# A seven-product output projection for the first half of a hybrid decoder block

## The chip, the core and the metric

The kernel runs on one core of a Trainium2 chip. The core has TensorE (matrix products into PSUM), VectorE (DVE), ScalarE (ACT), GpSimd (POOL), and SyncE (SP), which here issues every DMA. The metric is the time of one execution on the device, in microseconds; less is better. Times are medians of several runs. The profile is one further execution, recorded instruction by instruction; its times count from its first instruction.

## The reference

One decoder layer over 2048 positions of width 1024, in float32:

```python
h = rmsnorm(x, norm1_g)
p_q, p_k, p_v, p_g, p_a, c_b, c_c, c_h = split(h @ w_in)
o_gla  = rmsnorm(gla_chunked(q, k, v, log_a), gla_norm_g) * silu(p_g)   # 512 columns
o_conv = c_b * causal_depthwise_conv(c_c * c_h, conv_w)                 # 512 columns
x = x + concatenate([o_gla, o_conv]) @ w_out                            # 1024 x 1024
h2 = rmsnorm(x, norm2_g)
x = x + (silu(h2 @ w_ffn_gate) * (h2 @ w_ffn_up)) @ w_ffn_down
return rmsnorm(x, norm_f_g)
```

`gla_chunked` is a causal gated linear attention with a state carried from chunk to chunk.

## The kernel before

**Precision.** TensorE multiplies a rounded form of float32. Each operand is therefore split into a high part and the rest: ACT writes the high part, DVE subtracts (`split`, L146 and L147). A product of two split operands is three matmuls: high by high, high by rest, rest by high (L328 to L330 in `product_step`).

**Seven products.** The positions are in four blocks of 512, two to a half. The large projections are done half by half in units. A unit takes a 2x2 arrangement of weight tiles (A11 to A22) and a 2x2 arrangement of operands: B11 and B12 are the first half of the depth for the two blocks, B21 and B22 the second. Instead of eight products it does seven, on sums and differences of weights (S1 to S4, made by POOL in `unit_weights`) and of operands:

- T1 = B12 - B11, T2 = B22 - T1, T3 = B22 - B12, T4 = B21 - T2.
- The order is A11 B11, S1 T1, S2 T2, A12 B21, S3 T3, S4 B22, A22 T4 (`PRODUCTS`).

At a depth of 1024 a product is four steps of 128, so twelve matmuls, and a unit 84. Of its four results three are collected in SBUF by ACT copies (L348) and DVE adds (L352); the fourth stays in PSUM.

**Stages.** In order: statistics and operands of half 0; input projection of half 0 (twelve units); input projection of half 1 (twelve units); output projection of half 0; output projection of half 1; then the FFN of each half. The operands of half 1 (28 of them, 512 KB each with both parts) are made in the background of the input projection of half 0 by `h1_ahead` and stored in DRAM (`s_h1`); `load_pairs` loads them when the second input projection begins. The pool `opp` holds 28 operands.

**The output projection** (`out_proj`, from L712) is plain: for each pair of output tiles, eight depth steps of 128, each with three matmuls for each tile and block (L722, L723, L725), so 384 for a half. Its operands are the GLA and conv results, split and stored as pairs (`s_gla`, `s_mix`), loaded by `build_mix`. DVE adds the residual, the sum is stored in `s_x1`, and `sum_squares` (L703, L704) gathers the statistics of the next norm. The residual tiles, the unit's copies and the squares come from one pool of nine buffers (`tp`).

**Order of the work.** `tick()` is called after every product, and after every depth step of the plain output projection. Every second tick takes one step from the queue `background` (gate, GLA chunks, operands of half 1); a flag `hurry` makes it every tick at the start. If a generator is in `ahead`, it gets a step at every fourth tick; before the FFN nothing is in it. A GLA chunk is three steps: scores, finish of the chunk before, outputs. `gla_half(0)` mostly runs in the input projection of half 1, `gate(1)` behind it, and `gla_half(1)` from there into the output projection. GLA tiles, gate tiles and operands under way share the pool `bx` of eleven buffers of 128x512. The set `done` names finished chunks, of each half only the last.

A planner simulates the program while it is built. It orders each engine's instructions, the DMA issues of SP included, by the times at which it expects them to be ready, and gives out buffers as they come free. On the chip each engine, and SP's queue, then goes through its instructions in that order.

The change touches the ends of these functions and the driver:

```python
for r, j, c, _ in next(units):                 # conv results, L568
    y = cc[r, j]
    dve.tensor_tensor(y[:], c[:], y[:], ALU.mult)
    hi = tp.tile([P, PB], F32R, name="hi", tag="t")
    split(y[:], hi[:], y[:].bitcast(F32R))
...
drain_background(lambda: (1, PT - 1) in done)  # driver, L980
ssq = out_proj(0, build_mix(0))
```

## Time and profile before

| | |
|---|---|
| median of 3 runs | 2166.09 us |
| lowest, highest | 2165.67, 2172.95 us |
| the profiled execution | 2172.21 us, span 2170.2 us |
| granted TensorE clock in it | 0.983 |
| TensorE busy | 95% |
| DVE, ACT, POOL busy | 67%, 46%, 46% |
| moved by DMA | 467.65 MB, 215 GB/s |

A row of the groups of instructions names the line, the engine, the operation, the tile it writes and those it reads, the shapes and the count; behind the bar stand the busy time in microseconds and the mean of one in nanoseconds, and then the idle time of the engine before them with what ended it. A row by stretch gives the stretch, its length, and for each engine the busy time and the number of instructions, then the granted clock, the share of the 16 DMA engines and GB/s. A row of the chain of waits gives a start, a length, and what the chain ran through. A DMA row ends with the median time from issue to landing. PE is TensorE's matmuls, PEld its weight loads.

### The profile page before, as it was taken

What the parts mean: (1) busy time and instruction counts of PE and PEld (TensorE: products, weight loads), DVE (VectorE), ACT (ScalarE), POOL (GpSimd) and SP (SyncE); (2) the same over time, 40 slices, a digit from 0 to 9 for tenths busy, and PEclk for the clock granted to TensorE, in tenths of its full rate; (3) what the DMA queues carried; (4) which work ended last, traced back from release to release, by engine and by line L of the source; (5) the groups of instructions that cost most, each with busy time, mean ns of one, the idle gap of its engine ahead of it and who ended that gap; (6) DMA issues with size and microseconds to landing.
All of it is one profiled execution on the core that took longest, in us unless ns stands there. A gap on an engine that the chain in (4) does not pass through costs nothing.

```text
span 2170.2 us, 26909 instructions
## 1 busy us (share of the span) xinstructions
PE 2055.1 (95%) x9133; PEld 1658.8 (76%) x9133; DVE 1447.5 (67%) x2034; ACT 1009.1 (46%) x1960; POOL 993.6 (46%) x714
## 2 busy tenths in 40 slices
PE   4899999999999999999999999998999999999896
PEld 3577787887888887788888877787888888876675
DVE  8849965557774486787887565554656666576654
ACT  4555434564543334554555453333444545463344
POOL 4526422212201374555555337774545444447774
PEclk9999999999999999999999999999999999999998
DMA  3259668532576882565555677698343534688772
GB/s 148 73 197 317 217 239 276 153 116 89 169 274 214 334 306 97 187 244 194 217 215 184 227 304 263 240 342 326 125 167 136 184 136 149 229 331 328 292 276 107
DMA packets 189978, 467.65 MB, mean 215 GB/s; under 512 B 19856, under 2 KB 65168, under 8 KB 180112
## 3 DMA queue, kind: packets, MB, share of 16 engines
q1 hardware_dynamic: 189840, 465.93, 59.5%
q8 instruction: 72, 1.18, 0.2%
q14 instruction: 66, 0.54, 0.1%
HBM read 297.03 MB, written 168.82 MB: 215 GB/s over the span
## 4 chain that ended last, share of the span: by engine, by line
PE 71%; DVE 11%; DMA 8%; issue 4%; ACT 3%; POOL 3%; SPq 1%; DVEq 0%; POOLq 0%; ACTq 0%
PE mm L328 21%; PE mm L330 21%; PE mm L329 20%; DVE wq L147 2%; DVE h L440 2%; DMA op<-sa_T 2%; PE mm L722 2%; PE mm L725 2%; PE mm L723 2%; DMA raw<-in_wdown_dram 1%; DVE op L147 1%; DMA op<-sa_B 1%; DVE so L147 1%; ACT wq L146 1%; DVE c L352 1%
## 5 line engine op out<-in xcount | busy, mean ns | idle before, releaser
L328 PE MATMUL mm<-op,wq 128*128 128x512 f32 x2495 | 987.7, 398 | 38.6 <-ACT c L348 18.2
L330 PE MATMUL mm<-op,wq 128*128 128x512 f32 x2495 | 972.0, 394 | 18.8 <-DVE wq L147 18.0
L329 PE MATMUL mm<-op,wq 128*128 128x512 f32 x2495 | 981.0, 393 | 4.1 <-DVE op L147 4.1
L147 DVE TENSOR_TENSOR wq<-raw,wq 128x512 fp32r<-128x512 f32 (+2 forms) x628 | 532.1, 854 | 345.0 <-ACT wq L146 338.9
L146 ACT ACTIVATE wq<-raw 128x512 fp32r<-128x512 f32 (+2 forms) x628 | 365.2, 587 | 583.4 <-PE mm L330 408.5
L328 PEld LDWEIGHTS mm<-op,wq 128*128 128x128 f32 x2495 | 473.4, 190 | 159.1 <-ACT c L348 25.4
L330 PEld LDWEIGHTS mm<-op,wq 128*128 128x128 f32 x2495 | 473.4, 190 | 130.4 <-DVE wq L147 30.7
L329 PEld LDWEIGHTS mm<-op,wq 128*128 128x128 f32 x2495 | 473.4, 190 | 102.3 <-DVE op L147 5.1
L313 POOL TENSOR_TENSOR raw<-s,raw 128x512 f32<-128x512 f32 (+2 forms) x98 | 131.8, 1345 | 473.6 <-DVE wq L147 442.8
L352 DVE TENSOR_TENSOR c<-mm,c 128x512 f32<-128x512 f32 x270 | 185.2, 686 | 101.2 <-PE mm L330 98.5
L311 POOL TENSOR_TENSOR s<-raw 128x512 f32<-128x512 f32 (+2 forms) x98 | 131.0, 1337 | 197.7 <-DMA raw<-in_wffn_dram 87.5
L318 POOL TENSOR_TENSOR raw<-raw 128x512 f32<-128x512 f32 (+2 forms) x98 | 129.9, 1326 | 128.9 <-DVE wq L147 119.8
L348 ACT ACTIVATE c<-mm 128x512 f32<-128x512 f32 x270 | 156.7, 585 | 31.3 <-PE mm L330 30.2
L312 POOL TENSOR_TENSOR raw<-raw 128x512 f32<-128x512 f32 (+2 forms) x98 | 138.0, 1409 | 4.7
L704 POOL TENSOR_TENSOR ssx<-ssx,q 128x512 f32<-128x512 f32 x52 | 75.7, 1467 | 136.4 <-ACT q L703 136.1
L884 POOL TENSOR_TENSOR y<-c,y 128x512 f32<-128x512 f32 x66 | 98.9, 1500 | 72.4 <-DVE c L352 68.9
L147 DVE TENSOR_TENSOR so<-t,so 128x512 fp32r<-128x512 f32 x100 | 87.9, 885 | 26.0 <-ACT so L146 25.8
L146 ACT ACTIVATE wq<-s 128x512 fp32r<-128x512 f32 (+2 forms) x98 | 57.5, 587 | 94.5 <-PE mm L330 91.8
L722 PE MATMUL mm<-op,wq 128*128 128x512 f32 x256 | 101.1, 395 | 0.0
L723 PE MATMUL mm<-op,wq 128*128 128x512 f32 x256 | 99.8, 390 | 0.0
L147 DVE TENSOR_TENSOR wq<-s,wq 128x512 fp32r<-128x512 f32 (+2 forms) x98 | 77.6, 792 | 17.0 <-ACT wq L146 16.4
L146 ACT ACTIVATE so<-t 128x512 fp32r<-128x512 f32 x100 | 62.8, 629 | 42.8 <-DMA sa_T<-so 17.6
(177 smaller groups left out, 1922.8 us busy)
## 6 DMA issues: line engine op xcount, KB each, us to landing
raw<-in_wffn_dram SPq DMA_DIRECT2D x44, 1024.0 KB, 5.4
sa_T<-so SPq DMA_DIRECT2D x88, 512.0 KB, 4.7
op<-sa_T SPq DMA_DIRECT2D x88, 512.0 KB, 9.8
sa_B<-so SPq DMA_DIRECT2D x69, 512.0 KB, 3.4
op<-sa_B SPq DMA_DIRECT2D x69, 512.0 KB, 9.6
raw<-in_win_dram SPq DMA_DIRECT2D x24, 1024.0 KB, 5.3
raw<-in_wdown_dram SPq DMA_DIRECT2D x24, 768.0 KB, 6.6
sx<-y SPq DMA_DIRECT2D x48, 256.0 KB, 3.5
```

Of the source, the lines that this page charges most:

```text
L146: last_hi[:] = [act.activation(hi, src, AF.Copy)]
L147: return dve.tensor_tensor(lo, src, hi.bitcast(F32), ALU.subtract)
L311: pool.tensor_tensor(s1, a21, a22, ALU.add)
L312: pool.tensor_tensor(a21, a11, a21, ALU.subtract)
L313: pool.tensor_tensor(a11, s1, a11, ALU.subtract)
L328: pe.matmul(o[:], wh, xh, start=first and k == 0, stop=False, skip_group_check=True)
L329: pe.matmul(o[:], wh, xl, start=False, stop=False, skip_group_check=True)
L330: return pe.matmul(o[:], wl, xh, start=False, stop=k == n - 1, skip_group_check=True)
L348: act.activation(t[:], o[:], AF.Copy)
L352: dve.tensor_tensor(t[:], o[:], t[:], ALU.add)
L722: pe.matmul(o[e, j][:], wh, m[:, 0, :], start=k == 0, stop=False)
L723: pe.matmul(o[e, j][:], wh, m[:, 1, :], start=False, stop=False)
```

## The change

The first half's output projection is done by `unit`, in four units of seven products. For this the first half's conv and GLA results are stored as plain values (`s_val`), one 128x512 tile for each block and depth step. The generator `mix_ahead` reads them back, makes the differences on POOL, splits them, and stores the 28 operands in `s_mixp`. It is put into `ahead` before the input projection of half 1, and while `often` is set it gets every odd tick. Finished GLA chunks are now all entered in `done`; the generator waits there for block 0 and then for block 1. After the input projection the rest of the generator is run, the 28 operands are loaded, and `out_first` does the four units. `unit_weights` takes the output weights in the layout they have (`mixed`), with the quarters as strided views. The output projection of half 1 is as before.

```diff
-    pace, ahead, hurry = [0], [], []
+    pace, ahead, hurry, often = [0], [], [], []
...
         if pace[0] % 2 == 0 or hurry:
             step()
-        elif ahead and pace[0] % 4 == 1:
+        elif ahead and (pace[0] % 4 == 1 or often):
             next(ahead[0], None)
...
     def weight_quarter(src):
-        n = src.shape[-1]
+        n = src.shape[-1] if len(src.shape) == 2 else PB
         h = wqp.tile([P, 2, PB], F32R, name="wq", tag="wq")[:, :, 0:n]
-        split(src, h[:, 0, :], h[:, 1, :])
+        hi, lo = h[:, 0, :], h[:, 1, :]
+        if len(src.shape) == 3:
+            hi, lo = [y.rearrange("p (k c) -> p k c", c=P) for y in (hi, lo)]
+        split(src, hi, lo)
         return h
...
+        if mixed:
+            tiles = raw.rearrange("p a n -> p (a n)").rearrange("p (i k e c) -> p i k e c", i=2, k=4, e=2)
+            a11, a12, a21, a22 = [tiles[:, i, :, e, :] for e in range(2) for i in range(2)]
+            s1 = s1.rearrange("p (k c) -> p k c", c=P)
...
                 dve.tensor_tensor(y[:], c[:], y[:], ALU.mult)
+                if half == 0:
+                    store(s_val[j][4 + i0 + r][:], y[:])
+                    continue
                 hi = tp.tile([P, PB], F32R, name="hi", tag="t")
...
                 gla_finish(*chunks[n - 1], *o)
+                done.add(chunks[n - 1])
...
         dve.scalar_tensor_tensor(osb[:], ot[:], col(C_GN), g[:], ALU.mult, ALU.mult)
+        if b < 2:
+            for h in range(HEADS):
+                store(s_val[b][h][:, t * P : (t + 1) * P], osb[:, h, :])
+            return
         split(osb[:], g[:].bitcast(F32R), osb[:].bitcast(F32R))
...
+    def mix_ahead():
+        def put(n, k, h):
+            hi, lo = [bx[0].tile([P, PB], F32R, name=e, tag="b") for e in ("hi", "lo")]
+            split(h[:], hi[:], lo[:])
+            for e, y in enumerate((hi, lo)):
+                store(s_mixp[n][k][:, e, :], y[:].bitcast(F32))
+
+        def fetch(j, k):
+            h = bt("h")
+            load(h[:], s_val[j][k][:])
+            return h
+
+        for n, j, k0 in (("B21", 0, 4), ("B22", 1, 4), ("B11", 0, 0)):
+            while n == "B11" and (0, PT - 1) not in done:
+                yield
+            h = fetch(j, k0)
+            yield
+            for k in range(4):
+                cur = h
+                if k < 3:
+                    h = fetch(j, k0 + k + 1)
+                put(n, k, cur)
+                yield
+        while (1, PT - 1) not in done:
+            yield
+        for k in range(4):
+            b11, b12 = fetch(0, k), fetch(1, k)
+            yield
+            b22, b21, t1 = fetch(1, 4 + k), fetch(0, 4 + k), bt("t1")
+            pool.tensor_tensor(t1[:], b12[:], b11[:], ALU.subtract)
+            put("T1", k, t1)
+            yield
+            pool.tensor_tensor(t1[:], b22[:], t1[:], ALU.subtract)
+            put("T2", k, t1)
+            yield
+            pool.tensor_tensor(b12[:], b22[:], b12[:], ALU.subtract)
+            put("T3", k, b12)
+            yield
+            pool.tensor_tensor(t1[:], b21[:], t1[:], ALU.subtract)
+            put("T4", k, t1)
+            yield
...
+    def out_first(ops):
+        ssq = [tiny.tile([P, PB], F32, name=f"ssx{j}", tag=f"ssx{j}", bufs=1) for j in range(2)]
+        begun = set()
+        for d0 in range(0, KD, 2):
+            ys = {}
+            for e in range(2):
+                for j in range(2):
+                    ys[e, j] = tt("y")
+                    load(ys[e, j][:], xt[j, :, d0 + e, :])
+            for e, j, c, p in unit(wout[d0 // 2], ops, mixed=True):
+                y = ys[e, j]
+                (dve if p else pool).tensor_tensor(y[:], y[:], c[:], ALU.add)
+                store(s_x1[j][d0 + e][:], y[:])
+                sum_squares(ssq[j], y[:], j not in begun)
+                begun.add(j)
+        return ssq
...
     background.append(gate(1, ops))
+    ahead.append(mix_ahead())
+    often.append(True)
     in_proj(1, ops, None)
     drain_background(lambda: (1, PT - 1) in done)
-    ssq = out_proj(0, build_mix(0))
+    for _ in ahead.pop():
+        pass
+    often.clear()
+    ssq = out_first(load_pairs(s_mixp))
```

More of the change, by code (lines that the diff above doesn't have):

```diff
@@ L104, in tile_hymba_block @@
     s_mix = [[dram.tile([P, 2, PB], F32, name=f"sm{b}_{k}") for k in range(4)] for b in range(NB)]
+    s_val = [
+        [dram.tile([P, PB], F32, name=f"sw{b}_{k}") for k in range(KD)] for b in range(2)
+    ]
+    s_mixp = {
+        n: [dram.tile([P, 2, PB], F32, name=f"sy{n}_{k}") for k in range(4)] for _, n in PRODUCTS
+    }
     s_gla = [dram.tile([P, HEADS, 2, PB], F32, name=f"sgla{b}") for b in range(NB)]
@@ L303, in raw_weights, with unit_weights @@
         return raw
-    def unit_weights(src):
+    def unit_weights(src, mixed=False):
         raw = raw_weights(src)
@@ L330, in product_step, with unit @@
         return pe.matmul(o[:], wl, xh, start=False, stop=k == n - 1, skip_group_check=True)
-    def unit(src, ops, into=None):
-        w = unit_weights(src)
+    def unit(src, ops, into=None, mixed=False):
+        w = unit_weights(src, mixed)
         def mul(i, o=None):
```

## The prediction

> **What bounds the kernel now.** I read the page's busy shares first, then the groups of instructions with shapes kept apart, then busy time by stretch around the change.
>
> ```profile
> PE 2055.1 (95%) x9133; PEld 1658.8 (76%) x9133; DVE 1447.5 (67%) x2034; ACT 1009.1 (46%) x1960; POOL 993.6 (46%) x714
> ```
>
> ```profile
> L328 PE MATMUL mm<-op,wq 128*128 128x512 f32 x2495 | 987.7, 398 | 38.6 <-ACT c L348 18.2 <-ACT wq L146 8.7 <-DMA op<-shT 4.0
> L722 PE MATMUL mm<-op,wq 128*128 128x512 f32 x256 | 101.1, 395 | 0.0
> ```
>
> ```profile
> core 0: us, PE busy (x) PEld busy (x) DVE busy (x) ACT busy (x) POOL busy (x), PEclk, DMA share, GB/s
> 173.00:280.00 107.00, 99.23 (x421) 79.12 (x420) 99.81 (x125) 50.03 (x90) 55.52 (x34) 0.98 0.76 259
> 322.00:629.00 307.00, 300.22 (x1559) 243.60 (x1560) 201.53 (x392) 165.44 (x392) 62.28 (x45) 0.99 0.52 170
> 629.00:730.00 101.00, 100.58 (x507) 83.11 (x506) 38.99 (x83) 35.72 (x94) 13.86 (x10) 1.00 0.83 286
> 730.00:818.00 88.00, 88.00 (x386) 72.24 (x385) 70.71 (x78) 34.54 (x61) 54.42 (x35) 1.00 0.86 304
> ```
>
> TensorE sets the end: 95% busy, and where the change lies its idle time is small. 322 to 629 is the second half's input projection, 629 to 730 the first half's output projection (101 us, 0.4 idle), 730 to 818 the second half's. 173 to 280 matters too: there the kernel already prepares 28 operands in the background, with DVE 93% busy. A matmul of 128x512 is listed with 395 ns, but its neighbours overlap it. The stretch from 730 holds almost nothing else: 88 us for 386, 0.228 us each; the chain of waits agrees, with two in 0.45 to 0.46:
>
> ```profile
> 701.15 0.46 PE mm L725 x2
> 729.72 0.45 PE mm L725 x2
> ```
>
> The Trainium skill (TensorE: Matmul & The Clock Gate, Back-to-back issue gap) states 131 ns as the sustained spacing at N=512; the saving below would then be 6.3 us. The trace disagrees, with 228 ns.
>
> **The change, part by part.**
>
> *Matmuls.* Each of the three lines of the output projection has 256 records, 768 for two halves, 384 a half. Seven products of four 128-deep steps with three matmuls are 84 a unit; four units make 336. So 48 go: 48 x 0.228 = **-10.9 us**. The GLA matmuls that run between them stay: 101 - 384 x 0.228 = 13 us.
>
> *Splits that go from the first half.* The conv results and the GLA outputs of the first half are stored as plain values.
>
> ```profile
> L147 DVE TENSOR_TENSOR c<-c,hi 128x512 fp32r<-128x512 f32 x16 | 14.5, 913 | 1.7 <-ACT hi L146 1.4
> L147 DVE TENSOR_TENSOR osb<-osb,gt 128x512 fp32r<-128x512 f32 x16 | 12.4, 772 | 5.2 <-ACT gt L146 4.8
> ```
>
> ```profile
> 264.13 2.43 DVE c L147 x2
> 268.33 0.59 ACT c L348
> 268.96 0.50 PE mm L328
> ```
>
> Eight of each sixteen go. The chain runs through two of the conv splits at 264 and then through the ACT copy that the next matmul waited for: 2.4 us on the path. I take **-2 us**, bounds 0 and -6 (the second conv group stores its halves among the GLA loads behind which TensorE waits at 345, below).
>
> *The background work.* 28 splits, 16 POOL differences, 32 loads of 256 KB and 56 stores of 256 KB enter the second half's input projection. The nearest rows are the same work for the input operands:
>
> ```profile
> L147 DVE TENSOR_TENSOR lo<-t,hi 128x512 fp32r<-128x512 f32 x12 | 12.2, 1015 | 1.3 <-ACT hi L146 1.3
> L146 ACT ACTIVATE hi<-t 128x512 fp32r<-128x512 f32 x12 | 7.6, 632 | 23.5 <-POOL t L240 10.0 <-DVE lo L147 5.3 <-POOL t L249 5.0
> L240 POOL TENSOR_TENSOR t<-h,t 128x512 f32<-128x512 f32 x12 | 19.0, 1581 | 12.4 <-DVE so L147 4.9 <-DVE op L147 3.7 <-DVE h L440 2.0
> L138 SPq DMA_DIRECT2D op<-siT x16: 319/319/320, 299.9 to 337.0; - x16
> ```
>
> DVE: 28 x 1.015 less 8 x 0.772 = +22 us; ACT 28 x 0.632 - 5 = +13; POOL 16 x 1.58 = +25; SP 88 issues x 0.32 = +28 (and a plain GLA chunk has four stores where it had two, eight chunks, +5, where eight conv stores go, -3). On 307 us DVE goes from 201.5 (66%) to 224 (73%), ACT from 54 to 58%, POOL from 20 to 28%. On average TensorE covers it. The pacing decides where it falls. A unit has seven ticks; odd ones step the GLA queue, even ones this generator: 42 turns in 84 ticks. The first half's 77 ticks give its queue 46 steps (16 at every tick, 30 at every second), 44 for what stands ahead of the first GLA, so two of GLA's 24 are done. A chunk is three steps: block 0 ends at tick 21, block 1 at tick 43. Ten turns go to B21 and B22, five to B11 (ticks 22 to 30), six are idle, twenty from tick 44 to 82 make the differences. All 35 fit; the loop that empties the generator afterwards finds nothing. If it did, each step would stand bare: POOL 1.6, ACT 0.6, DVE 1.0 us and its DMAs.
>
> Ticks 44 to 84 are this stretch:
>
> ```profile
> 500.00:629.00 129.00, 125.94 (x655) 101.80 (x654) 102.47 (x207) 65.99 (x163) 22.91 (x15) 1.00 0.48 156
> 527.00:555.00 28.00, 24.93 (x137) 19.95 (x136) 26.87 (x55) 13.37 (x36) 6.77 (x6) 1.00 0.45 138
> 605.00:629.00 24.00, 24.00 (x133) 19.71 (x130) 20.51 (x44) 12.31 (x35) 1.29 (x1) 1.00 0.78 272
> ```
>
> Sixteen splits add 16 us: DVE from 102 to 119 of 129, 92%. The preparation at 173 to 280, at 93%, lost 107 - 421 x 0.228 = 11 us of TensorE: that is the upper bound. The lower is 0, since ticks 2 to 30 fall where DVE has slack. Only 527 to 555 (26.9 of 28, +3) and 605 to 629 (20.5 of 24, +3) fill up, by 2 us and by nothing or 1; with ACT caught now and then behind a load I take **+3.5 us**.
>
> *Waits added on SP.* The first fetch of B11 (tick 22) and of the differences (tick 44) wait for the landing of the last GLA stores, issued a tick before. Behind them on SP stand GLA loads and the weights of later units.
>
> ```profile
> sgla<-osb SPq DMA_DIRECT2D x16, 256.0 KB, 2.8
> op<-siT SPq DMA_DIRECT2D x16, 512.0 KB, 7.6
> op<-siB SPq DMA_DIRECT2D x12, 512.0 KB, 8.6
> op<-sgla SPq DMA_DIRECT2D x16, 512.0 KB, 8.0
> siT<-hi SPq DMA_DIRECT2D x16, 256.0 KB, 6.0
> ```
>
> Such a store lands in 2.8 us; two raw weight buffers lead by up to a unit (25.6 us). Cost 0, upper bound 2 x 2.8, held in the 11 above.
>
> *The switch to the output projection.* Now 16 operands of 512 KB are loaded there; after, 28. The row for 28 is the switch to the second input projection:
>
> ```profile
> 299.00:322.00 23.00, 23.00 (x118) 18.43 (x118) 19.57 (x37) 11.01 (x27) 3.96 (x4) 1.00 1.01 403
> 322.00:351.00 29.00, 25.28 (x139) 20.73 (x140) 18.31 (x34) 13.46 (x36) 5.69 (x5) 1.00 0.93 342
> 629.00:653.00 24.00, 24.00 (x129) 19.71 (x128) 11.21 (x29) 10.76 (x34) 0.00 (x0) 1.00 0.96 340
> ```
>
> ```profile
> PE sc L622 <- issue: 3.7, 1, 3.7
> ```
>
> No operand was late there, but a GLA chunk's loads stood behind them, and TensorE lost 3.7 us at 345. The switch at 629 cost nothing. I take **+4 us**; lower bound 0. Upper: the 48 us from 605 move 24 x 0.272 + 24 x 0.340 = 14.7 MB; twelve more operands (6.3 MB) and three late pairs of stores (1.5 MB) make 22.5 MB, 61 us at the 370 GB/s of 299 to 351: 13 us.
>
> *Inside the four units.*
>
> ```profile
> L311 POOL TENSOR_TENSOR s<-raw 128x512 f32<-128x512 f32 x67 | 97.6, 1456 | 178.4 <-DMA raw<-in_wffn_dram 87.5 <-DVE wq L147 63.7 <-DMA raw<-in_win_dram 20.5
> L884 POOL TENSOR_TENSOR y<-c,y 128x512 f32<-128x512 f32 x66 | 98.9, 1500 | 72.4 <-DVE c L352 68.9 <-DMA y<-sx 3.4
> L704 POOL TENSOR_TENSOR ssx<-ssx,q 128x512 f32<-128x512 f32 x52 | 75.7, 1467 | 136.4 <-ACT q L703 136.1
> ```
>
> A unit takes 84 x 0.228 = 19.2 us. POOL gets 4 weight sums, 3 residual adds and 4 sums of squares: 4 x 1.46 + 3 x 1.5 + 4 x 1.47 = 16.2 us, 85%. DVE has seven weight splits (four before), three adds into copies and one residual add, under 10 us, ACT as much: TensorE covers them. The four residual tiles, three copies and the squares share nine buffers; a unit's first copy may wait for a store to land. The last sums of squares end some 4 us after the last unit, and the next projection asks for them three steps (8 us) in. **+1.5 us**, bounds 0 and 6 (1.5 us, one residual add, at each of four units).
>
> *Sum.* -10.9 - 2 + 3.5 + 4 + 1.5 = **-3.9 us**. The profiled execution took 2172.2 us (span 2170.2); it would take 2168.3. It stands 6.1 us above the median of the runs, 2166.1; from that, about **2163**.
>
> **Rivals.**
>
> *All hidden.* Only the gains stay: -12.9, **2153**. For it: TensorE's 0.4 us idle in 629 to 730. Against it: the losses at 173 to 280 and at 345 under the same kind of work.
>
> *The switch is bound by DMA.* It costs 13 us: +5.1, **2171**. For it: 403 and 340 GB/s at shares of 1.01 and 0.96. Against: no operand was late at 322 to 351. The Trainium skill (DMA: Bandwidth & Descriptors, Specifications) gives HBM about 358 GB/s a core; by that 22.5 MB take 63 us. The trace moved 403 GB/s for 23 us, so that limit does not hold here.
>
> *POOL slows DVE.*
>
> ```profile
> L147 DVE TENSOR_TENSOR wq<-raw,wq 128x512 fp32r<-128x512 f32 x4 | 2.7, 684 | 4.1 <-ACT wq L146 4.1
> L147 DVE TENSOR_TENSOR wq<-raw,wq 128x512 fp32r<-128x512 f32 x6 | 6.2, 1030 | 0.0
> ```
>
> The first row is of 629 to 653, POOL idle; the second of 192 to 214, POOL at work most of the time: the same split takes half as long again. POOL's 25 us in ticks 44 to 84 would stretch the DVE work beside it, 25 x 0.79 = 20 us, by up to 7: DVE at 126 of 129, and the loss of 11 in 107 becomes 13. Then +5.6, **2172**. The Trainium skill (GPSIMD Engine Reference, Specifications) says that POOL shares its SBUF interfaces with VectorE; by that rule, the trace agrees, 1030 against 684 ns. Against: POOL is busy only 48 of 129 us there.
>
> *Buffers make the differences late* (the other side). From tick 57 the second GLA shares eleven buffers with this generator, which holds up to seven. Thirteen of twenty steps are then left. A step may take two ticks, 2 x 307/84 = 7.3 us; alone it needs 1.6 + 0.6 + 1.0 + 6.0 (its store) = 9.2 us if its buffers must come back first. T4 of the last block is wanted six products into the first unit, about 25 us after its turn: 13 x (9.2 - 7.3) = 25, the point from which it decides. At 10.8 us a step the operands come 13 x 3.5 - 25 = 20 us late, all on TensorE: +16, **2182**. For it: more tiles wanted than there are. Against: steps overlap where buffers are free.
>
> **How the numbers follow.** Forecast 0.46 (its own range 2157 to 2169), all hidden 0.13, DMA 0.15, POOL on DVE 0.10, buffers 0.16. Half a per cent, 10.8 us, is about what a measurement tells from no change. Below 2155.3 lies most of "all hidden": 0.10. Above 2176.9 lie the buffers and the tails of the two middle cases: 0.20. The rest is 0.70. From 2153 to 2182 holds eight in ten.
>
> **What would show it.** Right: 336 matmuls at the seven-product lines in the output projection, at 0.228 us; about 90 us for it (76.6 and GLA's 13); TensorE idle 500 to 629 up by 3 to 4 us behind DVE splits, and 4 us at the switch behind GLA or operand loads; the conv wait at 268 gone. Wrong: TensorE waiting for T operands by several us (buffers), for operand DMAs at a share of 1 (DMA), POOL as releaser of weight splits in the four units, or the GLA chunks of the second half running past the projection.

## The result

The changed kernel takes 2206.6 us (median of 4 runs, 2200.33 to 2210.38), the kernel before in the same comparison 2167.5: a ratio of 1.0174 with an interval of 1.015 to 1.0198. It is slower by about 39 us, where 2163 was forecast and the range ended at 2182. The profiled execution took 2209.5 us (span 2207.8, before 2170.2), so it can stand for the runs.

The busy times of the page and the busy time by stretch, of the changed kernel; the stretches are those of the prediction, moved to where the stages now lie (input projection of half 1, output projection of half 0, output projection of half 1):

```profile
PE 2062.0 (93%) x9085; PEld 1660.1 (75%) x9085; DVE 1495.0 (68%) x2058; ACT 1027.4 (47%) x1996; POOL 1064.8 (48%) x758
```

```profile
318.00:648.00 330.00, 307.17 (x1558) 248.46 (x1558) 221.66 (x405) 171.48 (x409) 91.73 (x64) 0.96 0.64 215
648.00:764.00 116.00, 97.82 (x462) 76.91 (x461) 68.53 (x102) 49.44 (x117) 52.23 (x36) 0.93 0.78 271
764.00:853.00 89.00, 89.00 (x390) 72.99 (x389) 68.45 (x73) 32.64 (x56) 51.03 (x33) 1.00 0.90 328
```

The 48 matmuls are gone (9133 to 9085), yet the two stages of the change take 330 + 116 us where they took 307 + 101. The untouched third is as before. Two columns of the first two rows say how: TensorE now stands idle 23 and 18 us (before 6.8 and 0.4), and the granted clock falls from 0.99 and 1.00 to 0.96 and 0.93. The next view, what TensorE waited for, has its columns in this order: total us, times, longest. First the changed kernel in the two stages, one after the other, then the kernel before over both:

```profile
PE sc L640 <- DVE kq L630: 15.0, 2, 8.0
PE mm L342 <- ACT c L362: 4.4, 3, 2.4
PE sc L640 <- issue: 3.4, 2, 1.8
```

```profile
PE sc L640 <- DVE kq L630: 14.9, 2, 8.0
PE mm L342 <- DMA op<-syT: 1.6, 5, 0.4
PE mm L342 <- DMA op<-syB: 1.5, 5, 0.3
```

```profile
PE sc L622 <- issue: 3.7, 1, 3.7
PE sc L622 <- DVE kq L612: 1.9, 1, 1.9
PE mm L328 <- ACT c L348: 1.2, 1, 1.2
```

Four waits of 7 to 8 us carry the loss, at 349, 546, 659 and 696 us, all of one kind: the score matmuls of a GLA chunk (`sc`) wait for the decayed keys and queries (`kq`). No matmul of the projections waits long, and none waits for a new operand more than 0.4 us. What is late is the chunk that runs *between* the products.

Such a wait costs more than its length. Three stretches of the changed kernel, the first around the wait at 546 us (each row: the stretch, its length, TensorE busy; the granted clock stands third from the end):

```profile
540.30:550.50 10.20, 4.62 (x20) 3.96 (x21) 10.20 (x23) 3.28 (x8) 1.79 (x1) 0.51 0.59 171
629.00:636.00 7.00, 5.44 (x22) 4.08 (x22) 7.00 (x17) 3.47 (x8) 0.00 (x0) 0.53 0.97 362
668.00:688.00 20.00, 16.76 (x72) 10.20 (x71) 7.35 (x16) 6.40 (x19) 1.29 (x1) 1.00 1.03 409
```

With the idle time of 8 us goes a stretch of 10.2 us at half clock, which begins within it and lasts some 4 us beyond; with two of 2.5 and 1.6 us close together, one of nearly 7. What runs meanwhile takes twice as long: in the chain of waits a matmul at 548.6 us takes 0.43 us, one at 550.6 takes 0.23 (rows below). Over the input projection half clock lasts 27.3 us (before 3.4), over the output projection 17.1 (before 0). Its price can be read off. Within these stretches TensorE is busy 16.5 us in the input projection (before 3.4) and 8.5 us in the output projection (before 0), and at full clock half of that would do: some 6.5 and 4.3 us, an estimate. Idle time and half clock together leave 0.6 us of the one loss (23.1 - 16.0 - 6.5) and 3.2 us of the other (14.4 + 10.9 - 17.8 - 4.3). Part of this rest would be the last matmul before each gap, which no neighbour overlaps; it is not shown. The last row is the control: TensorE idle 3.2 of 20 us in ten pieces of some 0.3 us, with the clock at 1.00. The Trainium skill (TensorE: Matmul & The Clock Gate, Why this matters for your kernels) asks for no idle gap above about 3 us; the trace agrees, and shows that shorter gaps close together do it too. So did, once, a single idle time of 1.9 us at 435 us, with half clock from 437.6 to 441.0.

### The profile page after: what moved, and what is told of

The parts are those of the page before. It is cut to its first block, busy times and chain, and to the rows that moved or that the text cites. A ratio compares the mean times of both kernels' runs of the same rounds, so it can differ in the third digit from the quotient of the medians.

```text
span 2207.8 us, 27143 instructions
## 1 busy us (share of the span) xinstructions
PE 2062.0 (93%) x9085; PEld 1660.1 (75%) x9085; DVE 1495.0 (68%) x2058; ACT 1027.4 (47%) x1996; POOL 1064.8 (48%) x758
## 4 chain that ended last, share of the span: by engine, by line
PE 69%; DMA 12%; DVE 11%; issue 3%; ACT 2%; POOL 1%; SPq 1%; DVEq 0%; ACTq 0%; POOLq 0%
PE mm L342 22%; PE mm L344 21%; PE mm L343 21%; DVE wq L154 2%; DVE h L454 2%; DMA raw<-in_wdown_dram 2%; DMA op<-sa_T 1%; DMA op<-shT 1%; DVE lo L154 1%; DVE op L154 1%; DMA sw<-c 1%; DMA op<-sa_B 1%; DMA op<-syB 1%; PE a_ps L511 1%; DVE c L366 1%
## 5 line engine op out<-in xcount | busy, mean ns | idle before, releaser
L342 PE MATMUL mm<-op,wq 128*128 128x512 f32 x2607 | 1037.7, 400 | 41.7 <-ACT c L362 18.0
L344 PE MATMUL mm<-op,wq 128*128 128x512 f32 x2607 | 1016.3, 395 | 17.7 <-DVE wq L154 17.2
L343 PE MATMUL mm<-op,wq 128*128 128x512 f32 x2607 | 1026.5, 394 | 4.1 <-DVE op L154 4.1
L154 DVE TENSOR_TENSOR wq<-raw,wq 128x512 fp32r<-128x512 f32 (+2 forms) x636 | 542.5, 859 | 294.2 <-ACT wq L153 292.1
L342 PEld LDWEIGHTS mm<-op,wq 128*128 128x128 f32 x2607 | 496.6, 191 | 171.2 <-ACT c L362 25.6
L344 PEld LDWEIGHTS mm<-op,wq 128*128 128x128 f32 x2607 | 496.1, 190 | 134.0 <-DVE wq L154 28.5
L343 PEld LDWEIGHTS mm<-op,wq 128*128 128x128 f32 x2607 | 496.9, 191 | 106.5 <-DVE op L154 5.1
L327 POOL TENSOR_TENSOR raw<-s,raw 128x512 f32<-128x512 f32 (+2 forms) x102 | 138.2, 1354 | 486.7 <-DVE wq L154 472.8
L366 DVE TENSOR_TENSOR c<-mm,c 128x512 f32<-128x512 f32 x282 | 193.4, 686 | 113.4 <-PE mm L344 110.7
L325 POOL TENSOR_TENSOR s<-raw 128x512 f32<-128x512 f32 (+2 forms) x102 | 138.8, 1361 | 197.9 <-DMA raw<-in_wffn_dram 88.7
L332 POOL TENSOR_TENSOR raw<-raw 128x512 f32<-128x512 f32 (+2 forms) x102 | 136.5, 1338 | 118.0 <-DVE wq L154 102.8
L362 ACT ACTIVATE c<-mm 128x512 f32<-128x512 f32 x282 | 164.0, 586 | 28.2 <-PE mm L344 25.4
L326 POOL TENSOR_TENSOR raw<-raw 128x512 f32<-128x512 f32 (+2 forms) x102 | 144.9, 1421 | 5.1
L906 DVE TENSOR_TENSOR c<-c,c 128x512 f32<-128x512 f32 x66 | 69.0, 1045 | 0.0
L910 POOL TENSOR_TENSOR t<-c,c 128x512 f32<-128x512 f32 x44 | 59.5, 1352 | 5.0 <-DVE c L906 5.0
```

Of the source, the lines that this page charges most:

```text
L154: return dve.tensor_tensor(lo, src, hi.bitcast(F32), ALU.subtract)
L325: pool.tensor_tensor(s1, a21, a22, ALU.add)
L326: pool.tensor_tensor(a21, a11, a21, ALU.subtract)
L327: pool.tensor_tensor(a11, s1, a11, ALU.subtract)
L332: pool.tensor_tensor(a12, a12, a11, ALU.subtract)
L342: pe.matmul(o[:], wh, xh, start=first and k == 0, stop=False, skip_group_check=True)
```

## Where the time went: the stages

Stage lengths in us, from the first matmul of each stage to the first of the next, one profiled execution for each kernel; ratios are of medians to the runs of the kernel before on the same chip, each with its 95% interval.

| kernel | in. proj. half 0 | in. proj. half 1 | out. proj. half 0 | ratio |
|---|---|---|---|---|
| before | 295.1 | 307.1 | 101.1 | 1 |
| changed | 291.2 | 330.2 | 115.5 | 1.0174 [1.015, 1.0198] |
| `products_only` | 290.0 | 308.4 | 112.2 | 1.0095 [1.0071, 1.0118] |
| `products_16_loads` | 292.1 | 308.0 | 97.3 | 0.9983 [0.9972, 0.9993] |
| `mix_only` | 292.3 | 326.3 | 110.3 | 1.0147 [1.0126, 1.0168] |
| `mix_no_stores` | 292.0 | 321.3 | 100.8 | 1.0048 [1.0032, 1.0065] |
| `mix_in_place` | 290.9 | 319.3 | 100.8 | 1.0056 [1.0038, 1.0074] |
| `mix_no_pool` | 292.7 | 318.6 | 100.6 | 1.0055 [1.0037, 1.0072] |
| `mix_dma_only` | 293.0 | 311.8 | 100.6 | 1.0016 [1.0007, 1.0025] |
| `b_at_switch` | 291.9 | 324.4 | 112.2 | 1.015 [1.0128, 1.0172] |
| `b_at_switch_four_loads` | 293.9 | 319.5 | 110.4 | 1.0116 [1.0097, 1.0135] |
| `after_four_loads` | 290.7 | 324.8 | 112.6 | 1.0153 [1.0129, 1.0178] |
| `before_four_loads` | 295.6 | 302.2 | 100.5 | 0.999 [0.9974, 1.0006] |
| `before_bx10` | 294.5 | 309.8 | 100.5 | 1.0017 [1.0005, 1.003] |
| `products_late_y` | 290.8 | 307.8 | 139.6 | 1.019 [1.0175, 1.0205] |
| `products_act_loads` | 291.3 | 311.0 | 116.1 | 1.0106 [1.0083, 1.0129] |
| `after_act_loads` | 292.5 | 325.4 | 120.4 | 1.0173 [1.0152, 1.0193] |

The output projection of half 1 takes 88.8 us in all of them. From before to the changed kernel the span grows by 37.6 us: -3.9 in the first input projection, +23.1 in the second, +14.4 in the output projection, +4.0 in all later stages together, which nothing here explains. A stage length is that of one execution: the runs of the changed kernel lie up to 10 us apart and those of `mix_in_place` up to 9, and the profiled execution can stand near one end. So a difference of some 4 us between two rows can be that of two executions.

The causes that the expectations weigh: the order on SP's queue (theory Q there); the 28 operand loads at the switch (D); the buffers that the background work takes from the GLA chunks (B); the residual tiles' pool (T); and the engine work of the background itself (W). My theory from the trace was queue and buffers; the rivals were the others. No kernel here beats the one before by half a per cent; the nearest, at 0.9983, leaves work out.

## Experiments: the two halves of the change apart

**`products_only`: the seven products without the background work.**

```diff
-    ahead.append(mix_ahead())
-    often.append(True)
     in_proj(1, ops, None)
     drain_background(lambda: (1, PT - 1) in done)
-    for _ in ahead.pop():
-        pass
-    often.clear()
-    ssq = out_first(load_pairs(s_mixp))
+    ssq = out_first(load_pairs(s_h1))
```

> The changed kernel without the generator that prepares the operands; the four seven-product units multiply the input projection's 28 stored operand pairs in place of the mixed results, so the mixing is left out of the output. Theory Q (the GLA chunk's fourteen small loads stand on SP's one queue behind the generator's stores and the operand loads, and TensorE, which goes in order, waits at the scores): the 23 us that the second input projection gained go, the four units still lose one or two waits at the switch: 2163 to 2175. Theory D (the switch with its 28 operands is the loss): still 10 us above the kernel before, 2178. Theory B (the eleven shared buffers run out because the generator holds some): all of it goes, 2155.

Measured: 2184.3 us against 2165.1. The input projection is back at 308.4 us; the output projection stays long, 112.2. So the 23 us of the one stage belong to the background work, and 11 of the 14 of the other appear without it, from the switch on. The time lies above every range that was named, since the dearest theory of the switch reached 2178.

**`mix_only`: the background work without the products.** The output projection is the old one, on stand-in operands.

```diff
-    ssq = out_first(load_pairs(s_mixp))
+    pairs = [[s_h1[n][k % 4] for n in (("B11", "T1") if k < 4 else ("B21", "B22"))] for k in range(KD)]
+    ssq = out_proj(0, [[load_pair(p) for p in row] for row in pairs])
```

> The changed kernel with the generator, but the first half's output projection is the plain one of before, on sixteen operand pairs of the input projection in place of the mixed results. What the generator stores is not used, so the mixing is left out of the output. Theory Q and theory B: the input projection of the second half keeps its +23 us, waits at the GLA scores; 2183 to 2190. Theory D: the generator costs little by itself, 2165 to 2172.

Measured: 2195.6 us against 2165.1; the input projection takes 326.3 us, and the old output projection 110.3 in place of 101.1, although it loads 16 operands as before. The two halves alone cost 19.2 and 30.5 us, together 10.6 more than the change. In the output projection they cost 11.1 and 9.2 us alone and 14.4 together, so there they would delay the same things in part; that is argued from the sums. This time too lies above the ranges named (2183 to 2190 the highest).

## Experiments: the switch to the output projection

**`products_16_loads`: sixteen operand loads in place of 28.** `products_only` with twelve operands used twice.

```diff
-    ssq = out_first(load_pairs(s_h1))
+    ops = {n: [load_pair(p) for p in s_h1[n]] for n in ("B11", "T1", "T2", "B21")}
+    ops.update(T3=ops["T1"], B22=ops["B21"], T4=ops["T2"])
+    ssq = out_first(ops)
```

> The kernel with the products only, loading sixteen of its 28 operands and using the first twelve of them twice (the output is not the layer's). Theory D: the 22 us by which the four units exceed their 90 us go, 2160 to 2166. Theory T: the wait for the first copy stays, and so does most of the rest, 2176 to 2184.

Measured: 2164.1 us, and 97.3 us for the output projection: twelve loads of 512 KB cost 14.9 us there. The time is in theory D's range, though not all of the 22 us above 90 go, as it had them. What TensorE waited for from 318 to 764 us, first `products_only`, then `products_16_loads`; then a stretch of `products_only` after the switch, and its chain at the second of these waits (start, us, what):

```profile
PE sc L640 <- DVE kq L630: 12.2, 3, 6.7
PE mm L342 <- ACT c L362: 5.9, 2, 4.7
```

```profile
PE sc L640 <- DVE kq L630: 5.5, 2, 3.7
PE mm L342 <- ACT c L362: 4.4, 2, 3.2
```

```profile
640.00:657.00 17.00, 12.66 (x45) 9.36 (x45) 3.97 (x11) 3.69 (x9) 0.00 (x0) 0.90 1.03 411
```

```profile
632.91 10.04 DMA sm<-hi
...
642.98 0.61 ACT c L362
```

The DMA engines are full, 1.03 at 411 GB/s. The operands come in time; what was asked for beside or behind them doesn't: the store of a conv result lands after 10 us, so the buffer for a unit's copy is missing for 4.7; the next GLA chunk's loads leave SP at 652 where they left at 645 with sixteen loads, and its scores wait 6.7. Both would come of full engines, yet the chunk's loads feel them through SP's order: from 600 to 700 us SP stood 17.6 us at operand loads until an earlier one had landed, and 10.0 with sixteen. This edit takes away bytes and issues at once, so it doesn't separate the two.

**`b_at_switch`: twelve of the 28 loads at half the size.** The changed kernel, with its twelve B operands taken out of the background work; they are loaded as plain values of 256 KB at the switch and split there.

```diff
+    def load_split(src):
+        o = opp.tile([P, 2, PB], F32R, name="op", tag="op")
+        load(o[:, 1, :].bitcast(F32), src[:])
+        split(o[:, 1, :].bitcast(F32), o[:, 0, :], o[:, 1, :])
+        return o
...
-        for n, j, k0 in (("B21", 0, 4), ("B22", 1, 4), ("B11", 0, 0)):
...
+            ops[n] = [load_split(s_val[j][k0 + k]) for k in range(4)]
```

> Computes everything. The twelve operands B of the seven products are not made in the background: they are loaded as single precision, 256 KB each instead of 512, at the switch, and split there; the background work makes the sixteen differences only. If the switch goes with bytes: the first half's output projection takes about 105 us instead of 115.5, the second half's input projection 318 to 322 instead of 330, and the time is 2185 to 2192. If it goes with the number of loads or their order behind other waits: the output projection stays at 112 to 115 and the time is 2195 or more.

Measured: 2196.4 us against 2167.1 (the changed kernel: 39 above, this one 29). The output projection takes 112.2 us, not 105, as the second theory had it: with background work, bytes alone are not what makes the chunk late. SP's queue shows what else is, here in the changed kernel itself (start, us, issue), with what SP waited for from 600 to 700 us below:

```profile
638.84 0.32 SPq L148 DMA_DIRECT2D syT<-hi  x1
641.87 0.32 SPq L148 DMA_DIRECT2D syT<-lo  x1
...
648.21 1.14 SPq L148 DMA_DIRECT2D syT<-hi  x1
...
651.55 0.63 SPq L145 DMA_DIRECT2D kq<-sk  x1
652.28 0.60 SPq L148 DMA_DIRECT2D sgla<-osb  x1
652.97 0.60 SPq L148 DMA_DIRECT2D syT<-lo  x1
653.62 1.64 SPq L145 DMA_DIRECT2D kq<-sk  x3
```

```profile
SPq L145 <- DMA op<-syB: 9.9, 10, 1.8
SPq L145 <- DMA op<-syT: 8.1, 9, 0.9
SPq L148 <- ACT hi L153: 5.1, 2, 3.0
SPq L148 <- DVE lo L154: 3.2, 2, 2.6
```

The last differences and the last conv and GLA results are stored in one stretch. Each store waits on SP for its split; the loads of the GLA chunk, whose scores are due at 651, stand behind them and go out at 651.6 to 661. In `b_at_switch` SP stood 10.7 us at such stores, and the chunk waits 7.1 us there. So there are two causes that cover each other: the operand loads, which take the full engines and SP's queue when there is no background work, and the background's last stores on SP when there is.

The wait at 696 us is neither, for no background store stands ahead of it. There the chunk's loads stand on SP behind the last operand loads and the next unit's residual tiles:

```profile
673.75 4.16 SPq L145 DMA_DIRECT2D op<-syT  x4
678.82 4.17 SPq L145 DMA_DIRECT2D y<-in_xt_dram  x4
683.94 4.16 SPq L145 DMA_DIRECT2D kq<-sk  x4
688.45 1.01 SPq L145 DMA_DIRECT2D ee<-sd  x2
```

```profile
658.68 0.42 DVE L630 SCALAR_TENSOR_TENSOR kq<-kq,ee 128x256 f32<-128x256 f32 x1
694.09 1.48 DVE L630 SCALAR_TENSOR_TENSOR kq<-kq,ee 128x256 f32<-128x256 f32 x1
```

Four issues take 4.2 us there, with the DMA engines at 409 GB/s, and the scores were due at 689. The last loads of the chunk go out at 691, and then the two DVE instructions for `kq` take 1.2 and 1.5 us with POOL at work beside them, where the chunk before took 0.42 for each. By that difference just under 2 us of this wait of 6.9 would be POOL's, an estimate.

**`products_late_y`: the residual tiles asked for later.** `products_only` with this in `out_first`:

```diff
-                    ys[e, j] = tt("y")
-                    load(ys[e, j][:], xt[j, :, d0 + e, :])
             for e, j, c, p in unit(wout[d0 // 2], ops, mixed=True):
-                y = ys[e, j]
+                y = tt("y")
+                load(y[:], xt[j, :, d0 + e, :])
```

> The kernel with the products only (operands of the input projection, so the mixing is left out of the output), with each unit's residual tiles fetched after its products, not before them. Theory T (four residual tiles taken from the nine buffers before a unit's copies make the first copy and its matmul wait): the 4.7 us wait for the first copy goes, and the GLA loads stand ahead of the residual loads; 2170 to 2178 against 2184. Theory D (28 operand loads of 512 KB take the queue): 2181 to 2186, no change.

Measured: 2209.5 us against 2168.7, the output projection 139.6. That is above both ranges. Yet the two waits that the edit aimed at are shorter: no copy is waited for near 640 us, and the scores wait 1.6 us for 6.7, as the chunk's loads leave SP at 649.5 for 651.9. So the early residual tiles had a part in them. New waits take more: 9.0 us for weights, and 18.0 us for a copy. A residual tile asked for at 739.9 lands 9.6 us later, its add and its square on ACT follow, and behind that square the unit's next copy stands on ACT.

**`products_act_loads`: the GLA loads on ACT's queue**, one for each tile instead of four, so each input is kept as one tensor in DRAM. `products_only` with this:

```diff
-        for dst, src in ((kq, s_kq[b]), (e[:, 2:4, :], s_d[b]), (vt, s_v[b]), (g, s_g[b])):
-            for i, r in enumerate(src):
-                load(dst[:, i, :], r[:, s])
+        for dst, src in ((kq[:], s_kq[b]), (e[:, 2:4, :], s_d[b]), (vt[:], s_v[b]), (g[:], s_g[b])):
+            act.dma_start(dst, src[:, :, s])
```

> The kernel with the products only, its GLA chunks loaded by four DMAs on ACT's queue. Theory Q for the switch: the 6.7 us wait at the scores near 665 goes, the four units take 100 to 105 us in place of 112, 2168 to 2176. If the 28 operand loads hold the DMA engines and not only SP: 110 to 114 us, 2180 to 2186.

**`after_act_loads`: the same edit in the changed kernel.**

> The changed kernel with four loads a GLA chunk, issued on ACT's queue and not on SP's. Theory Q (they wait behind other DMAs on SP): the waits at the scores near 349, 545, 659 and 695 us go, 2165 to 2180. Theory B: they stay, since the loads wait for their buffers on any queue, 2190 to 2206, or worse where ACT waits with them.

Measured: 2189.8 and 2204.0 us, against 2169 for before: the first is no better than `products_only` (1.0106 and 1.0095, intervals that overlap), the second no better than the changed kernel. The first time is above both of its ranges, which end at 2176 and 2186, the second in theory B's. The output projection takes 116.1 and 120.4 us. TensorE's longest waits, of the one and the other:

```profile
PE o_ps L666 <- ACT vt L653: 16.0, 2, 13.4
```

```profile
PE sc L642 <- DVE kq L632: 37.5, 3, 19.9
```

On ACT's queue the loads wait as well, and ACT's copies stand behind them: in the first kernel ACT stands 18.8 us at a load until the store of a conv result has landed, in the second 6.2 and 9.3 us between loads. That SP's order alone makes the chunk late is refuted in this form; the edit puts the wait on another engine and doesn't remove it.

**`after_four_loads`, `before_four_loads`: four larger loads for each GLA chunk on SP** (the edit above with `load` in place of `act.dma_start`).

> The changed kernel with each GLA input kept as one tensor in DRAM, so that a chunk is loaded by four DMAs in place of fourteen; bytes, buffers and order of the program are the same. Theory Q: a chunk's loads take about 2 us of SP instead of 6.3, most waits at the scores (some 35 us with the slower clock after them) go: 2165 to 2180. Theory B: buffers come back as late as before, 2200 to 2208. Theory D: 2195 to 2207.

> The kernel before with the same four DMAs a chunk. Theory Q: only the one wait of 3.7 us at the scores near 345 us and 2 us near 534 can go: 2160 to 2166. Theories B and D: 2164 to 2169, no difference.

Measured: 2196.1 (1.0153, beside the 1.0174 of the changed kernel in another comparison, intervals that overlap) and 2163.5 us (0.999). The first is in the range for no gain (2195 to 2207). In the profiled executions the 3.7 us wait at 345 us of the kernel before is gone, the input projection 302.2 for 307.1; in the changed kernel the four waits for `kq` remain, 27.9 us in total. So fewer issues take away none of the four that the change made. That they take away the one of the kernel before is not shown: the order on ACT changed with them. The chunk's exponentials go at 344.9 us there, ahead of a copy at 346.0; in the kernel before they went at 346.8, behind the copy at 345.8.

**`b_at_switch_four_loads`: both.**

> As b_at_switch, with four loads for each GLA chunk instead of eight. The changed kernel took about 10 us less with that. If the two gains add, the time is 2175 to 2185; if both act on the same waits, it stays at 2185 to 2190.

Measured: 2190.1 us, ratio 1.0116. The loads of a chunk go from fourteen to four there (not from eight). It stands 23 us above before, `b_at_switch` 29; the intervals of the ratios just overlap, and the expected 2175 to 2185 isn't reached.

## Experiments: the background work in the input projection

The first four keep the old output projection of `mix_only`.

**`mix_no_stores`: the 56 stores of the background work left out.**

```diff
             split(h[:], hi[:], lo[:])
-            for e, y in enumerate((hi, lo)):
-                store(s_mixp[n][k][:, e, :], y[:].bitcast(F32))
```

> The kernel with the generator only, with its 28 splits and 16 differences but without the 56 stores of what they make. Theory Q (stores that wait for ACT and DVE stand on SP ahead of the GLA loads): the 19 us that the second input projection gained go, 2174 to 2180 against 2196. Theory W (the generator's work on ACT and DVE stands ahead of GLA's and the weights' work there): they stay, 2191 to 2196.

**`mix_in_place`: the same loads, stores and engine work, but no buffers of its own for the results** (hi, lo and t1 go).

```diff
-            hi, lo = [bx[0].tile([P, PB], F32R, name=e, tag="b") for e in ("hi", "lo")]
-            split(h[:], hi[:], lo[:])
+            act.activation(h[:], h[:], AF.Copy)
+            dve.tensor_tensor(h[:], h[:], h[:], ALU.subtract)
```

> The kernel with the generator only, whose ACT, DVE and POOL instructions are all there but write over the tile they read, so that no buffers for high part, rest and T are taken; the 32 loads and 56 stores stay. Theory W (the work on ACT and DVE costs): the second input projection stays near 324 us, 2185 to 2196 in all. Theory B (the buffers that the generator takes from GLA cost): it falls to about 312 us as without the work, 2170 to 2178.

**`mix_no_pool`: `mix_in_place` without the sixteen differences on POOL.**

```diff
-            pool.tensor_tensor(b11[:], b12[:], b11[:], ALU.subtract)
...
-            pool.tensor_tensor(b21[:], b21[:], b21[:], ALU.subtract)
```

> Leaves out part of the computation: as in mix_in_place the results of the background work go nowhere, and the sixteen differences on POOL are not made at all; the copies and splits on ACT and DVE and all the loads are as there. If POOL's use of the memory beside DVE makes the gate's work near 545 us late: the wait there falls from 7.95 us to about 4, the second half's input projection takes about 314 us instead of 319.3, and the time is about 2174. If it is the ACT and DVE work itself: the wait stays near 8, the stage near 319, and the time is 2179 to 2182.

**`mix_dma_only`: its loads and stores alone.**

```diff
-            act.activation(h[:], h[:], AF.Copy)
-            dve.tensor_tensor(h[:], h[:], h[:], ALU.subtract)
...
-            pool.tensor_tensor(b11[:], b12[:], b11[:], ALU.subtract)
```

> The kernel with the generator only, with its 32 loads and 56 stores but without splits and differences: each value is stored twice as it was loaded. Theory W: the 19 us go, 2174 to 2180. Theory Q, in that the stores wait for engines: they go as well, since these stores wait only for loads; in that the DMAs themselves take the queue: they stay, 2190 to 2196. Read with the kernel without stores.

**`before_bx10`: the kernel before with one buffer less**, `bufs=10` for `bufs=11` in the pool `bx`.

> The kernel before with ten shared buffers in place of eleven (nine do not suffice for GLA). Theory B: one buffer less makes GLA's loads late without any generator: the second input projection 8 to 15 us longer, 2173 to 2182. Theory W or Q: 2163 to 2170.

Measured: 2179.4, 2180.9, 2178.4, 2172.1 and 2172.1 us. The first is in theory Q's range, but by luck: only 5.0 us go in this stage, and 9.5 in the output projection. The second lies between its two theories. The third has the wait of its first theory (4.5) and the stage of its second (318.6), and ends just under that one's range. The last two are just outside every range. What TensorE waited for from 318 to 764 us, one row each of `mix_only`, `mix_no_stores`, `mix_in_place`, `mix_no_pool` and `mix_dma_only`:

```profile
PE sc L640 <- DVE kq L630: 17.1, 3, 7.9
```

```profile
PE sc L640 <- DVE kq L630: 15.0, 2, 8.0
```

```profile
PE sc L640 <- DVE kq L630: 11.6, 2, 8.0
```

```profile
PE sc L640 <- DVE kq L630: 8.1, 2, 4.5
```

```profile
PE sc L640 <- DVE kq L630: 7.3, 2, 3.7
```

Read from the bottom, with the stage lengths of the table. The loads and stores alone: 311.8 us, some 3.5 above the 308.0 to 308.4 of the kernels with no background work. The engine work in place: 319.3, +7.5. Buffers and stores to the full: 326.3, +7.0, of which 5.0 go with the stores (`mix_no_stores`, 321.3). The changed kernel's 330.2 has another 3.9 with the same work in this stage; that difference between two orders, each profiled once, I can't assign. Steps of 4 us in this sum are no larger than what two executions can differ by; the steps of 7 are, and the ratios rise the same way, 1.0016, 1.0056 and 1.0147, with their intervals apart.

The two long waits have different causes. At 349 us the wait is 7.0 to 7.5 with buffers of its own (the changed kernel, `mix_only`, `mix_no_stores`) and 3.7 without. With the work the GLA chunk's loads leave SP from 340 us on, without it from 323 on. That the loads of the operand values take buffers that were free is my reading; one buffer less without that work (`before_bx10`) leaves the wait at 3.7. And these 3.7 us are no matter of loads: in `products_only` the chunk's decays are asked for at 331.8 and land within 5.4 us, TensorE waits from 340.0 on, and ACT takes their exponentials only at 341.1, behind a copy of the product that had just ended and a weight split. In the kernel before the same three stand on ACT in the same order. Near 545 us the wait stays at 8.0 in place and falls to 3.7 only with the engine work gone. The chain there, of the changed kernel (start, us, what; the last is a matmul back at full clock):

```profile
538.76 1.32 POOL t L745
...
540.99 1.77 DMA vt<-sv
542.76 0.66 DVE wq L154
...
544.03 0.66 DVE c L579
...
545.16 0.33 DVE kq L629
545.49 0.35 DVE kq L630
545.88 1.22 PE sc L640 x8
...
548.57 0.43 PE mm L342
...
550.56 0.23 PE mm L344
```

It is a unit of the convolution, with the second half's gates beside it: DVE, 26.9 of 28 us busy before the change, takes the chunk's `kq` in its turn behind gate, conv and weight work, and a POOL difference holds a buffer for which a load of the chunk waits. ACT stood 6.3 us there for DVE's gate scan (L539) with the chunk's exponentials behind it, and SP stood from 534.4 to 538.7 at a store that waited for its split, with the chunk's decay loads behind it; but without the stores (`mix_no_stores`) the wait is still 8.0 us, so this order alone isn't it. Without the differences (`mix_no_pool`) it falls to 4.5, and POOL acts there through DVE too: in `mix_in_place`, where the differences hold no buffer of their own, one conv instruction (L577) takes 1.60 us at 530.8 with POOL at work and 0.47 at 538.8 with POOL idle. So 3.5 us of that wait go with POOL's work; but the stage takes 318.6 us for 319.3 and the time is the same, as a copy waits 3.0 us at 361 instead.

Of the 23 us, the twelve B operands make about 6 (`b_at_switch`, 324.4 for 330.2); the other 16 above 308 stay with the differences. With the 3.9 us just left open, and one execution of each, this is a rough division.

## Why the prediction was wrong

- **Matmuls, -10.9.** Right as a number: 48 records fewer, and at full clock the new lines take 0.23 us each. But it is a gain only while nothing else ends later; with sixteen loads the stage takes 97.3 us, 3.8 less than before, where 90 was forecast, and the time is 0.9983 of before. So even with the background work and twelve loads for nothing, the change is worth a sixth of a per cent.
- **Splits removed, -2.** Right in kind: the wait of TensorE for the ACT copies from 173 us on went from 2.8 to 0.8 us. The stage is 3.9 us shorter here, and 1.2 to 5.1 us in the other kernels with this part.
- **Background work, +3.5 (0 to 11): the step that failed most.** It measured +23.1. The work itself was sized well on the two busiest engines: DVE 201.5 to 221.7 us busy (+20 for +22), POOL +29 for +25, while ACT took +6 for +13. These groups of the changed kernel from 318 to 648 us make 26 us for 27 of the 28 splits:

```profile
L154 DVE TENSOR_TENSOR lo<-h,hi 128x512 fp32r<-128x512 f32 x16 | 13.2, 824 | 18.9 <-ACT hi L153 7.8 <-DMA syB<-hi 4.9 <-DMA sk<-c 3.8
L154 DVE TENSOR_TENSOR lo<-t,hi 128x512 fp32r<-128x512 f32 x11 | 12.8, 1163 | 3.7 <-ACT hi L153 2.8 <-DMA sgla<-gt 0.9
```

  The fault was to turn busy shares into a loss, by analogy with the preparation of the operands in the first half (11 us at 93%). That stretch lies ahead of the GLA chunks. Here three engines, eleven buffers and a queue all serve the chunks too, and a chunk that comes late stops TensorE for 7 to 8 us at a time, at few places. Of the two stretches I had singled out by their DVE share, 527 to 555 is indeed where one falls, at 8 us plus half clock, not 2.
- **Half clock.** It wasn't in the sum at all, although the kernel before shows it at its one long wait. In the two stages it adds some 10.8 us, an estimate, to 33.8 of idle time: a third.
- **Waits on SP, 0.** Wrong. The last fetches don't hurt; the last stores do, as they wait for splits in front of the chunk's loads (the rows of SP above). The pacing was counted in ticks, and in ticks all 35 turns fit; on the chip the last of the stores goes out at 653 us, 5 after the stage's end.
- **The switch, +4 (0 to 13).** Mis-sized: twelve loads cost 14.9 us, just above the upper bound, and the stage lies 25 us above 90. Its nearest row, the 3.7 us at 345, was read as loads that stood behind the operands; by the trace of `products_only` and the order on ACT it was exponentials behind a copy (above). "No operand was late" held again, and was the wrong question: what stands behind the operands is late.
- **Inside the units, +1.5.** POOL was no bound (47.6 of 100 us busy from 664 to 764). The copy that waits for a store to land, named there, measured 4.7 us in `products_only`, once.

Of the rivals, *the switch is bound by DMA* named a real part, with the right size and half of the mechanism. *POOL slows DVE* is right as a fact: in the four units a weight split beside POOL takes 1035 ns (684 alone). There no weight was waited for, so that rival's own price wasn't paid; what POOL slowed was other work of DVE, ahead of the waits at 546 (a conv instruction) and 696 us (`kq`). *Buffers make the differences late* had the wrong victim: the differences came within 0.4 us of their time, and the GLA chunk paid, for buffers and stores together. *All hidden* was furthest off. The chance of 0.20 for slower was too small because every case was priced by one wait, and the mechanisms add up: the operand loads 14.9 us, the engine work 7.5, buffers and stores 7.0, the background's loads and stores alone some 3.5. The sum itself gives 2162 (2166.1 - 3.9), where the text says about 2163; nothing hangs on that.

## What to carry to other kernels

Work that fits into idle engine time still isn't free when it shares in-order queues, buffers or a DMA queue with something that TensorE waits for: look for the consumer with the least slack (here the GLA chunk's `kq`), and follow what each added instruction stands ahead of there. Price every idle time of TensorE above some 3 us, and shorter ones close together, at its length and, as here, about a third more for the clock. A gain of 11 us in matmuls doesn't pay for twelve loads of 512 KB at a point where the DMA engines are already full.

## What I had not expected of the hardware

The clock: idle times of 7 to 8 us came with stretches of 6.8 or 10.2 us at half clock, those of 3.7 us with 3.4 or 6.8, all multiples of 3.4, while ten gaps of 0.3 us in 20 us left it at 1.00. The Trainium skill (TensorE: Matmul & The Clock Gate, What's actually happening) gives a free-running window of about 3.4 us, and the steps agree. The DMA engines carried 411 GB/s on one core at a share of 1.03, and a store of 256 KB, which landed in 2.6 us in the median of that kernel, then took 10.
